# Moving nine query steps of the latent heads to a later stretch of a transformer layer on one core

## The chip, the cores and the metric

The kernel runs on one core of a Trainium2 chip. The metric is the device time of one execution in microseconds, and lower is better. A core has a matrix engine (TensorE, PE in the profile, with its weight loads on a row of their own, PEld), a vector engine (DVE), a scalar engine (ACT), a general engine (GpSimd, POOL) and a sync engine (SP). Here SP issues all loads, POOL issues all stores to DRAM, and each engine takes its instructions in a fixed order.

## The reference, cut to what matters

One layer of a streaming encoder: 1072 new rows (32 sample rows, 16 learned rows, 1024 prompt rows) and 512 cached rows of width 1024, in single precision. One input projection feeds two groups of eight heads; then an output projection, a feed-forward net and a norm.

```python
q = (rms_norm(c_q, q_norm) @ w_uq).reshape(B, L, 8, 96)          # latent heads: queries
q_mla = jnp.concatenate([q[..., :64], rope(q[..., 64:], pos)], axis=-1)
k, v = expand_mla_kv(latent, k_rope, w_ukv)                       # latent heads: keys, values
o_a = attend(take(q_mla), k_mla, v_mla, MLA_SCALE, cid[None, :] <= q_cid[:, None])
o_b = attend(take(f_q), f_k, f_v, FOX_SCALE, idx[None, :] <= q_idx[:, None], fox_bias(take(cum), cum))
x = x + concatenate([o_a, o_b]) @ w_out
return x + (silu(h @ w_gate) * (h @ w_up)) @ w_down               # h = rms_norm(x, norm_ffn)
```

## The kernel before

Every product runs in three matmuls on operands that are split into a high and a low part (`split`, L66), each matmul with 128 rows of weights and up to 512 columns. The program has three stretches: the projections (to about 240 us), the attention (to about 690 us) and the second half of the output projection with the feed-forward net (to the end).

The attention takes the eight forgetting heads first (h = 8 to 15), then the eight latent heads (h = 0 to 7). `attention` (L725) handles a head in two halves: the scores of the query tiles 5 to 8 (called 5a, 8a and so on below: head number and a), then those of tiles 1 to 4 and 0 (b). Beside the scores of one half run the values of the half before (`values`, L619: transposes L651 and L627, the products L667, L668, L637), kept in `state["pend"]`; the tile-0 transposes (L627, five at a time) are the last transposes of a head and run in the first half of the head after it. Every second head ends with `finish_pair` (L684, transposes L706), which writes that pair's rows into the operands of the output projection.

Beside this work runs a filler, a generator that makes other products in small steps. It is called by `fill()` (L728) after every score tile and every value block, some 25 times a head. Each call adds `rate` to what is owed, and for each whole step owed one step is made.

- With the forgetting heads the filler is `latent_heads` (L445), 62 steps: 16 key steps (K, six matmuls of 396 columns), 26 value steps (V, six of 256), two steps that only load, and 18 query steps (Q, nine of up to 358). The Q steps come in six blocks of three, in the order 4, 5, 0, 1, 2, 3: blocks 4 and 5 are the part of the queries that is rotated (a chain of five vector operations, L517 to L522), blocks 0 to 3 the plain part of two heads each. Between the last V step and the first Q step the operand tiles A_hi and A_lo are loaded anew (L493 to L500).
- With the latent heads it is `out_half` (L537), 48 half steps (O, six matmuls of up to 358) of the output projection over the forgetting heads' rows. They read what `finish_pair` of heads 14 and 15 writes, so `fill` makes none in the first half of head 0.

The results of the K, V and Q steps go through small buffers to DRAM: a ring of six (three tiles `room`, two buffers each) and a seventh in the tail of A_lo. The rotated blocks use only three of them in turn, since the others hold the tables. At the start of head 15 the code drains the filler, then `masks()` (L780) loads the shared rotated keys and the mask rows into the third `room` tile, where buffers 4 and 5 of the ring lie, and then `fetch(0)` (L393) loads head 0's operands. Head 0's scores need both.

The program order given so far is not the order on the engines: a planner lays out each engine's queue when the program is built, taking what comes first in the program among what its own estimates say is ready. So work whose inputs come late is overtaken by work written behind it. All pools of the attention are small: one buffer for the filler's sums (`psF`), two for scores (`psS`), two sets of head operands.

Of the kernel before, what the change touches and what calls it, by code (L numbers as in the profile page):

```python
# [42 lines left out]
RING = 6  # L43
# [6 lines left out]
def trunk(ctx: ExitStack, tc: tile.TileContext, a):  # L50
# [390 lines left out]
    psO = B.enter_context(tc.tile_pool(name="psO", bufs=1, space=PSUM))  # L441
    psF = B.enter_context(tc.tile_pool(name="psF", bufs=1, space=PSUM))
    mixed = {}

    def latent_heads():  # L445

        def weights(name, m, K, n):
            stg, hi, lo = (wp.tile([128, 512], t, tag=g, name=g)[:, :K * n].rearrange("p (k n) -> p k n", k=K)
                           for t, g in ((F32, "wst"), (FR, "woh"), (FR, "wol")))
            load(stg, a[name][m])  # L450
            split(hi, lo, stg, pool)
            return hi, lo

        hi, lo = slot("A_hi"), slot("A_lo")
        l_hi, l_lo = (t[:, :2 * NK].rearrange("p (k t) -> p k t", k=2) for t in (hi, lo))
        for c0, n in KC:
            for j, t in enumerate((l_hi, l_lo)):
                move(t[:, :, c0:c0 + n], sL[:, :, j, c0:c0 + n].rearrange("k p t -> p k t"))
        turn = [0]

        def part():

            turn[0] = (turn[0] + 1) % (RING + 1)
            return ring[turn[0]] if turn[0] < RING else lo[:, 3 * T:3 * T + 792]

        def es(n):
            return part()[:, :2 * n].rearrange("p (j t) -> p j t", j=2)

        todo = [("w_uk", m, 2, 128) for m in range(4)] + [("w_uv", m, 2, 256) for m in range(2)]
        ws = [weights(*todo[0])]  # L470
        yield
        for m in range(6):
            if m + 1 < 6:
                ws.append(weights(*todo[m + 1]))
            w = ws[m]
            if m < 4:
                for c0, n in KC:
                    ps = psF.tile([128, 512], F32, tag="psF", name="psF")
                    mm3(ps[:, :n], lambda k: w[0][:, k], lambda k: w[1][:, k],
                        lambda k: l_hi[:, k, c0:c0 + n], lambda k: l_lo[:, k, c0:c0 + n], 2)  # L480
                    spill(es, sK[m, :, :, c0:c0 + n], ps[:, :n], n)
                    yield
            else:
                for k0, n in [(128 * i, 128) for i in range(4)] + [(PAST + t0, n) for t0, n in QT]:
                    ps = psF.tile([128, 512], F32, tag="psF", name="psF")
                    for k in range(2):
                        s_hi, s_lo = l_hi[:, k, k0:k0 + 128], l_lo[:, k, k0:k0 + 128]
                        pe.matmul(ps[:, :256], s_hi, w[0][:, k], start=(k == 0), stop=False)
                        pe.matmul(ps[:, :256], s_hi, w[1][:, k], start=False, stop=False)
                        pe.matmul(ps[:, :256], s_lo, w[0][:, k], start=False, stop=(k == 1))  # L490
                    spill_v(None, k0, 4 * (m - 4), ps[:n, :256], n, part()[:, :512].rearrange("p (h d) -> p h d", h=4))
                    yield
        hi, lo = slot("A_hi"), slot("A_lo")  # L493
        c_hi, c_lo = (t[:, :3 * T].rearrange("p (k t) -> p k t", k=3) for t in (hi, lo))
        move(c_hi, sCQ[:, :, 0].rearrange("k p t -> p k t"))
        move(c_lo, sCQ[:, :, 1].rearrange("k p t -> p k t"))

        trig = [f32(ring[i][:, :716].rearrange("p (j t) -> p j t", j=2)) for i in range(3)]
        for t, (c0, n) in zip(trig, CC):
            load(t[:, :, :n], a["trig"][:, :, c0:c0 + n])  # L500
        order = (4, 5, 0, 1, 2, 3)
        ws = [weights("w_uq", order[0], 3, 128)]
        yield
        for i, m in enumerate(order):
            if i + 1 < 6:
                ws.append(weights("w_uq", order[i + 1], 3, 128))
            w = ws[i]
            for cs, (c0, n) in zip(trig, CC):
                ps = psF.tile([128, 512], F32, tag="psF", name="psF")
                mm3(ps[:, :n], lambda k: w[0][:, k], lambda k: w[1][:, k],  # L510
                    lambda k: c_hi[:, k, c0:c0 + n], lambda k: c_lo[:, k, c0:c0 + n], 3)
                if m < 4:
                    spill(es, sQ[m, :, :, c0:c0 + n], ps[:, :n], n, SCALE)
                else:
                    turn[0] = max(turn[0], 3)
                    t1, t2 = (f32(ring[3][:, 358 * j:358 * j + 358]) for j in range(2))
                    act.activation(t1[:, :n], ps[:, :n], AF.Copy, scale=SCALE)  # L517
                    dve.stream_shuffle(t2[:, :n], t1[:, :n], [(i + 16) % 32 for i in range(32)])
                    dve.tensor_tensor(out=t2[:, :n], in0=t2[:, :n], in1=cs[:, 1, :n], op=ALU.mult)
                    dve.tensor_tensor(out=t1[:, :n], in0=t1[:, :n], in1=cs[:, 0, :n], op=ALU.mult)  # L520
                    dve.tensor_tensor(out=t1[:, :n], in0=t1[:, :n], in1=t2[:, :n], op=ALU.add)
                    spill(es, sQR[m - 4, :, :, c0:c0 + n], t1[:, :n], n)  # L522
                    if turn[0] == RING:
                        turn[0] = 3
                yield

    w_ring, w_next = [], [0]

# [8 lines left out]
    def out_half():  # L537

        hi, lo = (rows4(t) for t in mixed["B"])
        turn = 0  # L540
        out_weights(1)
        for m in range(8):
            out_weights(m + 2)
            w = w_ring[m]
            for c0, n in CC:
                turn = (turn + 1) % 8
                xt = f32(ring[turn // 2][:, 396 * (turn % 2):396 * (turn % 2) + 358])
                load(xt[:, :n], a["xT"][128 * m:128 * m + 128, c0:c0 + n])
                ps = psF.tile([128, 512], F32, tag="psF", name="psF")
                for k in range(4):  # L550
                    pe.matmul(ps[:, :n], w[0][:, k], hi[:, k, c0:c0 + n], start=(k == 0), stop=False)
                    pe.matmul(ps[:, :n], w[0][:, k], lo[:, k, c0:c0 + n], start=False, stop=False)
                    pe.matmul(ps[:, :n], w[1][:, k], hi[:, k, c0:c0 + n], start=False, stop=(k == 3))
                    if k == 1:
                        yield
                dve.tensor_tensor(out=xt[:, :n], in0=ps[:, :n], in1=xt[:, :n], op=ALU.add)
                put(sX2[128 * m:128 * m + 128, c0:c0 + n], xt[:, :n])
                yield

    def scores(h, ops, i, rs):  # L560
        t0, nq = QT[i][0], 128
# [158 lines left out]
        for g in gens:  # L720
            yield from g

    state = {"pend": iter(()), "n": 0}

    def attention(hs, filler, steps, last):  # L725
        rate, owed = steps / (25.0 * (len(hs) - 0.7)), [0.0]

        def fill():  # L728
            if last and h == hs[0] and grps[0][0] == 5:
                return  # L730
            owed[0] += rate
            while owed[0] >= 1:
                next(filler, None)
                owed[0] -= 1

        rs = raw = None
        for h in hs:
# [2 lines left out]
                heads[nxt] = 0  # L740
            ops, v = heads.pop(h)
            if h == hs[-1]:
                for _ in filler:
                    pass
                if not last:
                    masks()
            nops = fetch(nxt) if nxt in heads else None
            if h % 2 == 0:
# [2 lines left out]
                raw = st.tile([128, T], F32, tag="raw", name="raw", bufs=1)  # L751
            for grps in (((5, 6, 7, 8),), ((1, 2, 3, 4), (0,))):
                todo = [i for g in grps for i in g]
                P, done = {}, 0
                for j, i in enumerate(todo):
                    P[i] = scores(h, ops, i, rs)
                    fill()
                    while done < (j + 1) * state["n"] // len(todo):
                        next(state["pend"], None)
                        fill()  # L760
                        done += 1
                for _ in state["pend"]:
                    pass
                if nops is not None and len(grps) == 1:
                    heads[nxt] = (nops, fetch_v(nxt))
                gens = [values(h, v, [(i, P[i]) for i in g], raw) for g in grps]
                state["n"] = sum(len(g) + g[0] if g != (0,) else 1 for g in grps)
                if h % 2 == 1 and len(grps) == 2:
                    gens.append(finish_pair(h // 2, rs, raw))
                    state["n"] += 3  # L770
                state["pend"] = chain(*gens)
        for _ in filler:
            pass

    mixed["B"] = (slot("B_hi"), slot("B_lo"))

# [7 lines left out]
        move(B3[96:106], sMK[0:10])  # L784
        mixed["B3"] = B3

    attention(range(8, 16), latent_heads(), 62, False)
    mixed["A"] = (slot("A_hi"), slot("A_lo"))

    attention(range(0, 8), out_half(), 48, True)  # L790
    for _ in state["pend"]:
        pass
    B.close()
# [295 lines left out]
```

## Time and profile before

| what | value |
|---|---|
| median of three runs | 1538.38 us (1536.78 to 1539.22) |
| the profiled execution's own time, and its span | 1537.25 us, 1535.5 us |
| TensorE: matmul busy, weight load busy | 1493.0 us (97%), 1433.5 us (93%) |
| VectorE, ScalarE, GpSimd busy | 971.5 (63%), 591.4 (39%), 198.5 us (13%) |
| mean granted TensorE clock | 0.993 |
| stretch of the attention | about 240 to 690 us |

The span runs from the first to the last instruction. Matmuls are pipelined and their ends are modelled, so the start of one matmul and the start of the next tell more than the durations. A line such as L67, L68 or L121 is that of a helper, so groups are told apart by the tile's name: `psF<-A_hi,woh` is a K or Q step, `psF<-woh,A_hi` a V step, `psF<-B_hi,woh` an O step, `psS<-room,x` the third score product of a latent head, which reads the masks' tile.

### The profile page before, as it was taken

What the parts mean: (1) busy time and instruction counts of PE and PEld (TensorE: products, weight loads), DVE (VectorE), ACT (ScalarE), POOL (GpSimd) and SP (SyncE); (2) the same over time, 40 slices, a digit from 0 to 9 for tenths busy, and PEclk for the clock granted to TensorE, in tenths of its full rate; (3) what the DMA queues carried; (4) which work ended last, traced back from release to release, by engine and by line L of the source; (5) the groups of instructions that cost most, each with busy time, mean ns of one, the idle gap of its engine ahead of it and who ended that gap; (6) DMA issues with size and microseconds to landing.
All of it is one profiled execution on the core that took longest, in us unless ns stands there. A gap on an engine that the chain in (4) does not pass through costs nothing.

```text
span 1535.5 us, 24295 instructions
## 1 busy us (share of the span) xinstructions
PE 1493.0 (97%) x9317; PEld 1433.5 (93%) x9317; DVE 971.5 (63%) x1861; ACT 591.4 (39%) x1198; POOL 198.5 (13%) x331
## 2 busy tenths in 40 slices
PE   9999998999898999989999999999999999999996
PEld 8999997888787898979999999999999999999996
DVE  8874626787966776766855655555555555655547
ACT  7443436777655666654511111111111121111124
POOL 0343242422131211200000000000000000000001
PEclk9999999999999999999999999999999999999999
DMA  6689567778587686515111111111111111111003
GB/s 196 233 258 299 172 210 249 238 218 262 147 238 185 174 212 161 148 41 206 34 50 44 54 42 42 42 42 42 42 42 42 53 58 53 44 42 42 28 1 115
DMA packets 87636, 184.19 MB, mean 120 GB/s; under 512 B 9754, under 2 KB 52954, under 8 KB 87428
## 3 DMA queue, kind: packets, MB, share of 16 engines
q1 hardware_dynamic: 70592, 128.34, 28.8%
q0 software_dynamic: 16928, 54.29, 10.1%
q8 instruction: 74, 1.21, 0.3%
q14 instruction: 42, 0.34, 0.1%
HBM read 123.93 MB, written 58.67 MB: 119 GB/s over the span
## 4 chain that ended last, share of the span: by engine, by line
PE 88%; DVE 4%; ACT 3%; issue 2%; DMA 1%; POOL 1%; DVEq 0%; SPq 0%; POOLq 0%; ACTq 0%
PE psG L122 11%; PE psG L121 11%; PE psG L123 11%; PE psD L890 5%; PE psD L891 5%; PE psD L889 5%; PE psS L589 5%; PE psT L651 4%; PE psA L123 3%; PE psA L121 3%; PE psA L122 3%; PE po L667 2%; PE po L668 2%; PE psA L386 1%; PE psA L387 1%
## 5 line engine op out<-in xcount | busy, mean ns | idle before, releaser
L898 DVE TENSOR_TENSOR x<-psD,x 128x408 f32<-128x408 f32 (+1 forms) x496 | 236.2, 522 | 4.3 <-PE psD L891 4.3
L122 PE MATMUL psG<-B_lo,gh 128*128 128x408 f32 (+1 forms) x528 | 172.8, 327 | 0.0
L121 PE MATMUL psG<-B_hi,gh 128*128 128x408 f32 (+1 forms) x528 | 172.8, 327 | 0.0
L122 PE MATMUL psG<-A_lo,gh 128*128 128x408 f32 (+1 forms) x528 | 172.6, 327 | 0.0
L121 PE MATMUL psG<-A_hi,gh 128*128 128x408 f32 (+1 forms) x528 | 172.3, 326 | 0.0
L891 PE MATMUL psD<-ah,dl 128*128 128x408 f32 (+1 forms) x528 | 172.1, 326 | 0.0
L123 PE MATMUL psG<-B_hi,gl 128*128 128x408 f32 (+1 forms) x528 | 171.8, 325 | 0.0
L123 PE MATMUL psG<-A_hi,gl 128*128 128x408 f32 (+1 forms) x528 | 171.8, 325 | 0.0
L890 PE MATMUL psD<-al,dh 128*128 128x408 f32 (+1 forms) x528 | 171.7, 325 | 0.0
L889 PE MATMUL psD<-ah,dh 128*128 128x408 f32 (+1 forms) x528 | 170.9, 325 | 0.5 <-ACT ah L67 0.5
L878 ACT ACTIVATE sl<-sl 128x408 f32<-128x408 f32 (+1 forms) x66 | 33.1, 503 | 351.3 <-DVE sl L877 351.2
L882 DVE TENSOR_TENSOR sq<-psG,rb 128x408 f32<-128x408 f32 (+1 forms) x66 | 35.0, 530 | 156.5 <-PE psG L123 156.5
L68 DVE TENSOR_TENSOR ptl<-psT,pth 128x512 fp32r<-128x512 f32 x192 | 104.6, 552 | 28.7 <-ACT pth L67 26.6
L592 DVE TENSOR_REDUCE nm<-psS 128x1 f32<-128x656 f32 (+2 forms) x144 | 104.0, 724 | 27.2 <-PE psS L589 25.6
L67 ACT ACTIVATE pth<-psT 128x512 fp32r<-128x512 f32 (+4 forms) x208 | 99.2, 480 | 55.7 <-PE psT L651 46.5
L830 POOL TENSOR_TENSOR acc<-acc,sq 128x408 f32<-128x408 f32 x10 | 10.8, 1076 | 812.4 <-ACT sq L829 811.9
L877 DVE TENSOR_TENSOR sl<-psG,rb 128x408 f32<-128x408 f32 (+1 forms) x66 | 34.9, 530 | 123.0 <-PE psG L123 123.0
L67 ACT ACTIVATE ah<-sl 128x408 fp32r<-128x408 f32 (+1 forms) x66 | 33.2, 503 | 197.2 <-DVE sl L883 125.8
L589 PE MATMUL psS<-b,a 128*128 128x328 f32 (+4 forms) x360 | 99.9, 331 | 7.4 <-ACT pb L597 6.1
L889 PEld LDWEIGHTS psD<-ah,dh 128*128 128x128 f32 x528 | 99.2, 188 | 0.9 <-ACT ah L67 0.7
L122 PEld LDWEIGHTS psG<-B_lo,gh 128*128 128x128 f32 x528 | 99.2, 188 | 0.5 <-issue 0.3
L121 PEld LDWEIGHTS psG<-B_hi,gh 128*128 128x128 f32 x528 | 99.2, 188 | 0.5 <-issue 0.2
(274 smaller groups left out, 3803.5 us busy)
## 6 DMA issues: line engine op xcount, KB each, us to landing
sg<-w_gu SPq DMA_DIRECT2D x44, 512.0 KB
a<-sQ SPq DMA_DIRECT2D x56, 268.0 KB
b<-sK SPq DMA_DIRECT2D x32, 396.0 KB
sg<-w_down SPq DMA_DIRECT2D x22, 512.0 KB
v<-sV SPq DMA_DIRECT2D x16, 512.0 KB
wst<-w_in SPq DMA_DIRECT2D x13, 512.0 KB
sV<-vt POOLq DMA_DIRECT2D x24, 256.0 KB, 4.5
sK<-room POOLq DMA_DIRECT2D x14, 396.0 KB, 4.9
```

The lines of the kernel that those rows point to most:

```text
L67: first = act.activation(hi, src, AF.Copy)
L68: return first.ins, eng.tensor_tensor(out=lo, in0=src, in1=f32(hi), op=ALU.subtract).ins
L121: pe.matmul(ps, whi(k), rhi(k), start=(k == 0), stop=False)
L122: pe.matmul(ps, whi(k), rlo(k), start=False, stop=False)
L123: last = pe.matmul(ps, wlo(k), rhi(k), start=False, stop=(k == K - 1))
L589: pe.matmul(out, qa[:K, t0:t0 + nq], kb[:K, k0 + c:k0 + c + w], start=(j == 0), stop=last)
L592: dve.tensor_reduce(out=nm[:nq, j:j + 1], in_=src, axis=AX.XY if len(src.shape) == 3 else AX.X, op=ALU.max, negate=True)
L651: pe.transpose(out=pt[:, 128 * g:128 * g + 128], in_=tiles[g][1][:, c:c + 128], identity=ident)
L889: pe.matmul(ps, dh[:, m], ah[:, cs], start=first and j == 0, stop=False)
L890: pe.matmul(ps, dh[:, m], al[:, cs], start=False, stop=False)
L891: pe.matmul(ps, dl[:, m], ah[:, cs], start=False, stop=last and j == len(parts) - 1)
L898: dve.tensor_tensor(out=x2[:, m, cs], in0=ps[:, :n], in1=x2[:, m, cs], op=ALU.add)
```

## The change

`latent_heads` now also yields the cost of what it has made: 1 for a step, 0 at two marks. The first mark (`state["keys"]`) stands after block 0, the second (`state["made"]`) after the last block. At the start of head 15 the filler is drained only up to the first mark; then come `masks()` and `fetch(0)` as before, and the nine steps of blocks 1, 2 and 3 are left to the paced filler of heads 15 and 0. From the first mark on the ring leaves out buffers 4 and 5. The rate of the forgetting heads follows from 53 steps in place of 62, that of the latent heads from 57 in place of 48. The filler of the latent heads is the rest of `latent_heads` and then `out_half`; in the first half of head 0 it may now run, but not past the second mark. `fill` makes a step as soon as anything is owed, not when a whole step is. The new tiles A_hi and A_lo, which `finish_pair` of heads 0 and 1 writes, are asked for in the second half of head 1.

```diff
         def part():
             turn[0] = (turn[0] + 1) % (RING + 1)
+            if state["keys"] and turn[0] in (RING - 2, RING - 1):
+                turn[0] = RING
             return ring[turn[0]] if turn[0] < RING else lo[:, 3 * T:3 * T + 792]
...
             w = ws[i]
+            if i == 3:
+
+                state["keys"] = True
+                yield 0
             for cs, (c0, n) in zip(trig, CC):
...
-                yield
+                yield 1
+        state["made"] = True
+        yield 0
...
         def fill():
-            if last and h == hs[0] and grps[0][0] == 5:
-                return
             owed[0] += rate
-            while owed[0] >= 1:
-                next(filler, None)
-                owed[0] -= 1
+            while owed[0] > 0:
+                if last and h == hs[0] and grps[0][0] == 5 and state["made"]:
+                    owed[0] = 0
+                    return
+                owed[0] -= next(filler, 1)
...
             if h == hs[-1]:
-                for _ in filler:
-                    pass
-                if not last:
+                if last:
+                    for _ in filler:
+                        pass
+                else:
+                    while not state["keys"]:
+                        next(filler)
                     masks()
...
                 todo = [i for g in grps for i in g]
+                if last and h == hs[1] and len(grps) == 2:
+                    while not state["made"]:
+                        next(filler)
+                    mixed["A"] = (slot("A_hi"), slot("A_lo"))
...
-        for _ in filler:
-            pass
...
-    attention(range(8, 16), latent_heads(), 62, False)
-    mixed["A"] = (slot("A_hi"), slot("A_lo"))
-
-    attention(range(0, 8), out_half(), 48, True)
+    first = latent_heads()
+    attention(range(8, 16), first, 53, False)
+
+    attention(range(0, 8), chain(first, out_half()), 57, True)
```

## Rows read from the trace of the kernel before

**Rows 1.** The page's busy time by engine, with shares of the span and instructions.
```profile
PE 1493.0 (97%) x9317; PEld 1433.5 (93%) x9317; DVE 971.5 (63%) x1861; ACT 591.4 (39%) x1198; POOL 198.5 (13%) x331
```
**Rows 2.** Busy time by stretch; columns as in the first line, all in us.
```profile
core 0: us, PE busy (x) PEld busy (x) DVE busy (x) ACT busy (x) POOL busy (x), PEclk, DMA share, GB/s
300.00:340.00 40.00, 39.75 (x291) 35.83 (x290) 32.25 (x67) 31.41 (x82) 12.31 (x25) 1.00 0.76 218
371.00:392.00 21.00, 19.35 (x124) 15.46 (x124) 15.72 (x31) 15.90 (x39) 2.41 (x8) 1.00 1.07 316
392.00:432.00 40.00, 35.41 (x207) 30.27 (x207) 37.12 (x74) 23.07 (x55) 11.32 (x16) 0.96 0.52 142
432.00:461.00 29.00, 26.95 (x174) 24.43 (x173) 16.88 (x36) 17.64 (x45) 11.06 (x18) 1.00 0.85 249
461.00:482.00 21.00, 16.65 (x94) 14.37 (x93) 11.45 (x22) 10.78 (x27) 4.10 (x7) 0.92 0.78 197
482.00:630.00 148.00, 145.11 (x946) 132.59 (x946) 104.88 (x198) 94.24 (x222) 30.84 (x54) 1.00 0.70 182
631.00:658.00 27.00, 26.57 (x176) 24.58 (x175) 18.02 (x34) 15.26 (x37) 5.67 (x10) 1.00 0.38 104
658.00:676.00 18.00, 16.51 (x108) 14.32 (x108) 14.31 (x28) 13.35 (x33) 0.54 (x1) 1.00 0.08 26
676.00:690.00 14.00, 9.80 (x57) 7.71 (x56) 9.71 (x21) 6.73 (x16) 1.84 (x6) 0.88 0.09 24
```
**Rows 3.** TensorE in order of time: the last V step, two heads' ends, the first Q step.
```profile
368.94 0.28 PE L490 MATMUL psF<-woh,A_lo 128*128 128x256 f32 x1
...
371.50 0.76 PE L627 MATMUL psT<-ident,pa 128*112 128x128 f32 x5 [0.79 <-DVE ptm L656]
...
387.67 0.41 PE L121 MATMUL psF<-A_hi,woh 128*128 128x358 f32 x1
...
390.61 0.72 PE L627 MATMUL psT<-ident,pa 128*112 128x128 f32 x5
```
**Rows 4.** TensorE: where the second, seventh, ninth and eighteenth Q steps begin.
```profile
395.03 0.33 PE L121 MATMUL psF<-A_hi,woh 128*128 128x358 f32 x1
...
422.72 0.43 PE L121 MATMUL psF<-A_hi,woh 128*128 128x358 f32 x1
...
430.46 0.34 PE L121 MATMUL psF<-A_hi,woh 128*128 128x356 f32 x1
...
459.17 0.43 PE L121 MATMUL psF<-A_hi,woh 128*128 128x356 f32 x1 [0.19 <-DVE room L144]
```
**Rows 5.** The SP queue in order of time: loads for head 0, and the masks.
```profile
438.32 1.95 SPq L61 DMA_DIRECT2D a<-sQ  x3
...
440.88 0.44 SPq L61 DMA_DIRECT2D a<-sQ  x1
...
459.40 1.24 SPq L61 DMA_DIRECT2D room<-sKR  x3
```
**Rows 6.** SP's longest wait from 425 to 475 us: total, times, longest.
```profile
SPq L61 <- DMA sQ<-room: 13.7, 2, 8.2
```
**Rows 7.** TensorE behind the last Q step, and at head 0's first scores.
```profile
460.73 0.39 PE L667 MATMUL po<-pth,v 128*128 128x512 f32 x1
...
469.01 0.43 PE L551 MATMUL psF<-B_hi,woh 128*128 128x358 f32 x1 [1.25 <-ACT B_hi L713]
...
469.89 0.32 PE L589 MATMUL psS<-room,x 106*128 106x328 f32 x1
```
**Rows 8.** TensorE: a V step and what follows it; two O half steps and what follows.
```profile
304.34 0.28 PE L488 MATMUL psF<-woh,A_hi 128*128 128x256 f32 x1
...
305.04 0.60 PE L651 MATMUL psT<-ident,pb 128*128 128x128 f32 x4
...
655.78 0.43 PE L551 MATMUL psF<-B_hi,woh 128*128 128x356 f32 x1
...
657.84 0.34 PE L589 MATMUL psS<-room,x 106*128 106x392 f32 x1
```

More of the change, by code (lines that the diff above doesn't have):

```diff
@@ L443, in trunk @@
     mixed = {}
+    state = {"pend": iter(()), "n": 0, "keys": False, "made": False}
     def latent_heads():
@@ L481, in latent_heads @@
                     spill(es, sK[m, :, :, c0:c0 + n], ps[:, :n], n)
-                    yield
+                    yield 1
             else:
@@ L491, in latent_heads @@
                     spill_v(None, k0, 4 * (m - 4), ps[:n, :256], n, part()[:, :512].rearrange("p (h d) -> p h d", h=4))
-                    yield
+                    yield 1
         hi, lo = slot("A_hi"), slot("A_lo")
@@ L502, in latent_heads @@
         ws = [weights("w_uq", order[0], 3, 128)]
-        yield
+        yield 1
         for i, m in enumerate(order):
@@ L524, in latent_heads @@
                         turn[0] = 3
-                yield
+                yield 1
+        state["made"] = True
+        yield 0
     w_ring, w_next = [], [0]
@@ L554, in out_half @@
                     if k == 1:
-                        yield
+                        yield 1
                 dve.tensor_tensor(out=xt[:, :n], in0=ps[:, :n], in1=xt[:, :n], op=ALU.add)
                 put(sX2[128 * m:128 * m + 128, c0:c0 + n], xt[:, :n])
-                yield
+                yield 1
     def scores(h, ops, i, rs):
@@ L721, in chain @@
             yield from g
-    state = {"pend": iter(()), "n": 0}
     def attention(hs, filler, steps, last):
```

## The prediction

> **What bounds the kernel now.** The page's busy table comes first: TensorE is busy 97% of the span, no other engine over 63% [rows 1]. So in most stretches time goes only where TensorE idles, and the sum of its work is the same after the change: not one matmul is added or removed. The question is where it idles, and the busy time by stretch answers it [rows 2]. From 300 to 340 us and from 482 to 630 us, where a filler runs beside the heads, the weight loads are busy 35.83 of 40 and 132.59 of 148 us, 0.896 both times. I take 0.896 as a full TensorE; what a stretch has less, over 0.896, is lost time. So 371 to 392 loses 21 - 15.46/0.896 = 3.7 us, 392 to 432 loses 6.2, 432 to 461 loses 1.7, 461 to 482 loses 5.0, 631 to 658 nothing (-0.4), 658 to 676 loses 2.0 and 676 to 690 loses 5.4. The changed part thus holds some 16.6 us between 371 and 482, and the end of the attention 7.4.
>
> The queues in order of time tell what those losses are. The last V step is at 368.94 and the first Q step at 387.67 [rows 3]: 18.7 us without filler, while A_hi, A_lo, the tables and the weights are loaded anew. Then the six rotated steps run 5.5 us apart (second to seventh step, 395.03 to 422.72, five gaps) and the plain ones 3.2 us apart (ninth to eighteenth, 430.46 to 459.17, nine gaps) [rows 4]. VectorE is busy 37.12 of 40 us from 392 to 432 [rows 2]: the rotation's chain of operations stands among the softmax work. At 461 the forgetting heads have run out. Head 0's last operand is issued at 440.88, but the masks only at 459.40 [rows 5], since their tile is the ring's buffers 4 and 5, whose last stores are those of block 2; SP waited 8.2 us for such a store [rows 6]. Head 0's first product with the masks starts at 469.89, and TensorE idles around it, 1.25 us in one piece [rows 7].
>
> **The change, part by part.**
>
> *Where the steps go.* Some 25 calls a head make the rates 62, 48, 53 and 57 over 182.5: 0.340 and 0.263 a call before, 0.290 and 0.312 after. The last V step is the 43rd step: call 127 before, and 145 after, as a step now comes when anything is owed (42/0.290). These 18 calls are 0.7 of a head; a head without filler took 19.1 us (371.50 to 390.61) [rows 3], of which 16 were work, so the V steps end 11.4 to 13.4 us later; I take 12.5. Everything tied to them moves with them: loads of A, rotated steps, block 0, sQ for head 0. Of the nine plain steps about seven fall to head 15 and two to head 0 by count.
>
> *Gain at head 0.* After block 0 the ring skips buffers 4 and 5, so the masks wait for block 0's own first two stores, not for block 2. Head 0's operands then bound it: 440.88 + 12.5 = 453.4, some 455.5 with the landing. TensorE would be out of other work near 461 (the last Q step ended at 460.73) [rows 7]. By 455.5 the plain steps, 3.2 us apart from about 446 on (the tenth, at 430.46 + 3.2 + 12.5), have come to three or four; five or six are left to lie beside head 0's first scores, 1.56 us each (459.17 to 460.73) [rows 4, 7], 8 to 9 us of work where 5.0 us was idle. The stretch 461 to 482 also had a granted clock of 0.92 [rows 2], that is half clock for 0.16 of 21 us, 1.7 us of lost work. Recovered: 5.0 + 1.7 = 6.7 us at most, and nothing at least. Stretch 432 to 461, the same plain steps beside heads, loses 6%, so I leave 0.9 of some 15 us: -5.8 us.
>
> *Cost of thinner filling in heads 8 to 13.* At call 127 the changed kernel has made 37 steps (127 x 0.290) where 42 stood, so 5 V steps fewer, each 0.70 us (304.34 to 305.04) [rows 8]: 3.5 us of work. If TensorE is what limits those heads, the work is only moved and the cost is 0; if not, it is 3.5. A head without filler needs 19.1 us, one with 7.3 V steps 16 + 5.1 = 21.1 of TensorE, so it stays the limit; some bursts will miss. I take 0.8.
>
> *Cost at the end.* 48 half steps at 0.312 a call last 154 calls, six heads from the middle of head 0, so they end in the first half of head 6. Before they ended at 657.84, ten of them after 631, 1.03 us each (655.78 to 657.84, two) [rows 8]. Without them 631 to 658 holds 27 - 10.3 = 17 us of attention alone. A forgetting head without filler loses 3.7 of 21 us, 18%; latent heads, with three products a score, lose 2.0 of 18, 11% [rows 2], and part of that is the scores running out. So 0 to 3.0 us, and I take 1.6. The drain of five half steps at head 7 goes; it cost nothing, since 631 to 658 is full.
>
> *No change costed:* the stretch without filler (18.7 us, now beside head 14 in place of 13b and 14a) and the rotated steps (now beside head 15), 3.7 and 6.2 us as before. The new ring of five buffers for the nine plain steps has 5 x 3.2 = 16 us a turn against a longest SP wait of 8.2 us for a store [rows 4, 6], so it hides; without that cover it would cost a few us of waits at the filler. The marks and the early step issue nothing. The masks' and head 0's loads stand earlier in SP's queue; the loads behind them are those of head 1, not wanted for another 10 us. A_hi and A_lo for `finish_pair` are asked for later but used only in head 2.
>
> *How far matmul busy time can be trusted* is the Trainium skill's point in "Trainium Kernel Development and Optimization", Performance Expectations: matmul busy time is a bad measure because matmuls are pipelined, weight-load busy time a good one. This trace agrees: from 392 to 432 matmuls look 89% busy, weight loads 76% against 90% in a full stretch [rows 2]. By matmul busy time 461 to 482 would have 4.35 us to give in place of 5.0, and the whole 0.65 us less gain.
>
> **Sum.** -5.8 + 0.8 + 1.6 = -3.4 us. The profiled execution took 1537.25 us, of which the span is 1535.5; it would take 1533.85. The median of the runs shown is 1.13 us above it, so 1535.0 us, 0.22% under the 1538.38 of before. About 0.2% (3.1 us) is what a measurement can tell here, so the forecast lies at that edge.
>
> **Rivals.**
>
> *More than head 0 is repaired* (faster). The rotated steps no longer meet the pair's end of heads 12 and 13 (it falls into the stretch without filler), and VectorE, nearly full from 392 to 432, gets room. For it: the clock was 0.96 there, 1.6 us of lost work. Against it: the chain of a rotated step is the same and still behind softmax work. If half of 6.2 + 1.6 goes: 1535.0 - 3.9 = 1531.1.
>
> *The gain is given back at the end or halved at the start* (no change). If head 6 and 7 without filler cost 3.0 and a spell of half clock (676 to 690 shows 0.88, 1.7 us of 14, once the scores had run out [rows 2]), the sum is -5.8 + 0.8 + 4.7 = -0.3: 1538.1. If the planner puts the nine steps ahead of head 0 in place of beside it, as before, half of the 5.8 goes: -0.5, 1537.9. Against the first: 658 to 676 ran without filler at 1.00. "TensorE: Matmul & The Clock Gate", What's actually happening, of the Trainium skill has the clock throttled unless activity releases it, which speaks against a longer thin end; this trace shows no fall before the scores end.
>
> *The late chain decides* (slower). All of block 4, 5 and 0 now lies 12.5 us later, and head 0 waits for it. From the last V step to head 0's last issue took 440.88 - 368.94 = 72 us [rows 3, 5]. If that is longer beside head 15, because VectorE has 93% to do already [rows 2], TensorE finds neither scores nor a ready step. It decides from the point where the operands come after 461, some 6 us late: a pace of 6.6 in place of 5.5 us for the six rotated steps would do. Then nothing of the 6.7 us comes back, the 2.4 us of thinner filling and empty end stay, and each further us of lateness adds one: with 2.5, 1538.4 + 2.4 + 2.5 = 1543.3. For it: the stretch without filler costs the same, and the loads of head 15 may delay those of A.
>
> *The steps do not move:* if the planner's estimates let the nine steps run where they did, the masks still come earlier; that is the forecast with a smaller gain, within the second rival.
>
> **How the numbers follow.** Forecast 0.38, with 1532.5 to 1537 as its own range (0.27 of it faster, 0.11 within 0.2%); more repaired 0.19 (faster); given back 0.26 (0.23 the same, 0.03 slower); late chain 0.17 (0.14 slower, 0.03 the same). That is faster 0.46, same 0.37, slower 0.17. The range reaches past the second case's 1531.1 to 1529.5 and up to 1540.5, short of the late chain's 1543.3; what it leaves out is some 0.07 below and 0.12 above.
>
> **What would show it.** Right: the masks' load follows the store of block 0's second step; head 0's first product with the masks starts near 456 to 458, with Q steps among its scores; the stretch to the start of head 0's values has weight loads near 0.87; the last O half step comes in the first half of head 6. Wrong: idle time before `psS<-room` as before, or a gap between Q steps and head 0 with VectorE full; a clock under 1 between the last O step and the end of the scores; or a loss of over 2 us in heads 8 to 13.

## The result and the profile after

The changed kernel takes 1548.95 us (median of five runs, 1546.58 to 1553.02) against 1538.64 us for the kernel before in the same session: ratio 1.0068, 95% interval 1.0057 to 1.0079, so 10.3 us slower. The profiled execution took 1546.58 us, its span 1544.8; that is 9.3 us over the profiled execution of before.

The page's busy table shows the same work to within 3 us [rows 1]. So the time is idle time on TensorE, as the prediction argued, and again the question is where.

```profile
PE 1490.7 (96%) x9317; PEld 1430.6 (93%) x9317; DVE 971.0 (63%) x1861; ACT 591.0 (38%) x1198; POOL 199.4 (13%) x331
```

Busy time by stretch, after; columns as in the first line. The stretches are cut where the phases of the changed kernel begin, so they answer to [rows 2] as sums, not line by line.

```profile
core 0: us, PE busy (x) PEld busy (x) DVE busy (x) ACT busy (x) POOL busy (x), PEclk, DMA share, GB/s
300.00:340.00 40.00, 38.87 (x274) 34.18 (x275) 32.08 (x65) 29.75 (x77) 10.29 (x21) 1.00 0.77 212
371.00:386.00 15.00, 15.00 (x114) 13.76 (x113) 11.54 (x26) 11.42 (x32) 4.25 (x11) 1.00 0.63 181
386.00:411.00 25.00, 22.14 (x143) 17.55 (x141) 20.03 (x38) 19.17 (x47) 4.69 (x8) 1.00 1.06 305
411.00:446.00 35.00, 30.38 (x188) 25.52 (x187) 30.20 (x69) 21.10 (x53) 8.25 (x13) 1.00 0.51 142
446.00:476.00 30.00, 19.13 (x106) 16.32 (x105) 8.64 (x18) 7.46 (x16) 10.42 (x17) 1.00 0.90 274
476.00:488.00 12.00, 10.09 (x59) 8.50 (x57) 7.02 (x14) 7.38 (x19) 4.53 (x6) 1.00 0.67 216
488.00:624.00 136.00, 132.40 (x865) 122.44 (x865) 93.96 (x174) 81.86 (x193) 30.32 (x51) 1.00 0.69 173
649.00:676.00 27.00, 24.30 (x159) 21.21 (x158) 21.08 (x40) 19.14 (x45) 4.05 (x7) 1.00 0.21 56
676.00:692.00 16.00, 14.21 (x92) 11.61 (x93) 11.94 (x26) 11.54 (x31) 1.43 (x4) 1.00 0.01 2
```

With the prediction's measure (weight loads over 0.896 is what TensorE needed), 446 to 476 loses 30 - 16.32/0.896 = 11.8 us, the largest loss by far. From 371 to 488 the loss is -0.4 + 5.4 + 6.5 + 11.8 + 2.5 = 25.8 us. Before, 371 to 482 lost 16.6 us and 3.3 more by its lower clock, 19.9 [rows 2]. That is +5.9 us. From 488 to 624 nothing is lost.

TensorE in order of time, after:

```profile
370.78 0.76 PE L636 MATMUL psT<-ident,pa 128*112 128x128 f32 x5 [0.16 <-DVE ptm L665]
...
384.46 0.29 PE L493 MATMUL psF<-woh,A_lo 128*128 128x256 f32 x1
...
410.92 0.41 PE L121 MATMUL psF<-A_hi,woh 128*128 128x358 f32 x1
...
444.62 0.43 PE L121 MATMUL psF<-A_hi,woh 128*128 128x358 f32 x1 [0.18 <-ACT room L524]
...
446.19 0.40 PE L674 MATMUL po<-ptm,v 128*128 128x512 f32 x1
447.75 0.44 PE L121 MATMUL psF<-A_hi,woh 128*128 128x358 f32 x1 [1.16 <-DVE room L144]
...
449.34 0.66 PE L646 MATMUL po<-pth,v 112*128 112x96 f32 x5
...
454.19 0.43 PE L121 MATMUL psF<-A_hi,woh 128*128 128x358 f32 x1 [1.84 <-DVE A_lo L144]
...
471.64 0.43 PE L121 MATMUL psF<-A_hi,woh 128*128 128x358 f32 x1 [1.12 <-DVE room L144]
...
473.21 0.50 PE L598 MATMUL psS<-b,a 128*128 128x328 f32 x2
...
475.90 0.31 PE L598 MATMUL psS<-room,x 106*128 106x328 f32 x1
...
698.77 0.42 PE L858 MATMUL psG<-A_hi,woh 128*128 128x408 f32 x1 [1.36 <-DVE raw L721]
```

The last V step is at 384.46, where it was at 368.94 [rows 3]; the first Q step at 410.92 (387.67); the seventh, the first plain one, at 444.62 (422.72) [rows 4]. The forgetting heads' last products stand at 446.19 and 449.34. From there seven of the nine moved steps, the tenth to the sixteenth, run alone, one each 2.9 us (454.19 to 471.64, six gaps), for 1.7 us of matmuls. Only behind the sixteenth comes head 0's first product, at 473.21, and the first one with the masks at 475.90, 6 us later than before [rows 7].

What TensorE waits for from 446 to 476 (us in total, times, longest):

```profile
PE psF L121 <- DVE room L144: 7.9, 8, 1.4
PE psF L121 <- DVE A_lo L144: 3.0, 2, 1.8
```

There is one buffer `psF`: a step can't start until ScalarE has copied the sum of the step before and VectorE has split it. Beside attention work that wait is filled; alone it stands as 1.1 us a step, 10.9 us in all.

The SP queue after, the load of A_hi, two loads behind it, the masks and the last load that head 0's first scores need:

```profile
388.15 0.38 SPq L61 DMA_DIRECT2D A_hi<-sCQ  x1
...
397.31 8.34 SPq L61 DMA_DIRECT2D v<-sV  x4
405.75 0.37 SPq L58 DMA_DIRECT2D wst<-w_uq  x1
...
456.98 1.23 SPq L61 DMA_DIRECT2D room<-sKR  x3
...
460.78 0.58 SPq L61 DMA_DIRECT2D a<-sQ  x1
```

The same queue before (not shown so far), and below it TensorE's first product of the feed-forward net before:

```profile
369.13 0.38 SPq L61 DMA_DIRECT2D A_hi<-sCQ  x1
...
379.18 3.88 SPq L61 DMA_DIRECT2D v<-sV  x4
```

```profile
688.81 0.68 PE L845 MATMUL psG<-A_hi,woh 128*128 128x408 f32 x1 [1.10 <-DVE raw L712]
```

The masks now come 2.4 us earlier than before (456.98 against 459.40 [rows 5]), but the last operand 19.9 us later (460.78 against 440.88; eight loads `a<-sQ` start from 458.72 to 463.71, and in the program's order the first four are head 0's, the others head 1's). The feed-forward net starts 10.0 us later, and that accounts for the whole difference.

### The profile page after: what moved, and what is told of

It reads as the page before. It is cut to its first block, busy times and chain, and to the rows that moved or that the text cites. A ratio compares the mean times of both kernels' runs of the same rounds, so it can differ in the third digit from the quotient of the medians.

```text
span 1544.8 us, 24294 instructions
## 1 busy us (share of the span) xinstructions
PE 1490.7 (96%) x9317; PEld 1430.6 (93%) x9317; DVE 971.0 (63%) x1861; ACT 591.0 (38%) x1198; POOL 199.4 (13%) x331
## 4 chain that ended last, share of the span: by engine, by line
PE 87%; DVE 5%; ACT 5%; issue 1%; DMA 1%; SPq 0%; POOL 0%; DVEq 0%; ACTq 0%
PE psG L122 11%; PE psG L121 11%; PE psG L123 11%; PE psD L903 5%; PE psD L904 5%; PE psD L902 5%; PE psS L598 5%; PE psT L660 4%; PE psA L123 3%; PE psA L121 3%; PE psA L122 3%; PE po L676 2%; PE po L677 2%; ACT pb L606 1%; PE psA L386 1%
```

## The experiments

The main theory: the late chain decides. Everything from the last V step to head 0's operands comes later than the forgetting heads' work lasts. Rivals: the order in which the planner queues the nine steps ahead of head 0, the thinner filling of heads 8 to 13 and of the end, and the step made as soon as anything is owed.

**The chain early, the rest of the change kept.** 62 steps' pace again, with the filler held at the first mark until head 15.

```diff
             while owed[0] > 0:
+                if not last and state["keys"] and h != hs[-1]:
+                    owed[0] = 0
+                    return
...
-    attention(range(8, 16), first, 53, False)
+    attention(range(8, 16), first, 62, False)
```

> The changed kernel with the forgetting heads' pace put back to 62 steps, and the filler held at the first mark until head 15, so that the V steps end and A is loaded at the calls of before, and the same nine Q steps are left to heads 15 and 0. Late chain (head 0 waits for blocks 4, 5 and 0): the last V step is back near 369 us, no run of Q steps stands alone ahead of head 0, and the time falls by some 12 us, to 1535 to 1538. Thin filling of heads 8 to 13 as the cause: only the 4 us that those heads lost come back, 1545. The moved steps or the ring of five buffers as the cause: no change, 1547 to 1550.

Measured 1536.49 us, ratio 0.9990 (0.9979 to 1.0000): 12.5 us under the changed kernel, even with the kernel before or slightly faster. The first store of a rotated query (on POOL) comes at 403.56 where the changed kernel has 424.92, and head 0's first product with the masks at 459.08:

```profile
403.56 0.71 POOL L64 DMA_DIRECT2D sQR<-room  x1 [3.32 <-DVE nm L601]
...
459.08 0.39 PE L598 MATMUL psS<-room,x 106*128 106x328 f32 x1
```

So lateness, with the thinner filling that goes with it, is all of the slowdown.

**The end's pace.** The changed kernel with 49 for 57 in the latent heads.

```diff
-    attention(range(0, 8), chain(first, out_half()), 57, True)
+    attention(range(0, 8), chain(first, out_half()), 49, True)
```

> The changed kernel with the latent heads' pace at 49 steps in place of 57, so that the O steps end at head 7 and not in head 6. Late chain: only the end is repaired, 1.8 us, 1547. Empty end as the main cause: 1541 or less.

Measured 1546.43 us, ratio 1.0054 (1.0036 to 1.0071), 2.5 us under the changed kernel, though the two intervals overlap. The trace agrees: the last matmul of the O steps starts at 665.7 in place of 652.6, and 649 to 676 loses 27 - 23.52/0.896 = 0.75 us in place of 3.3:

```profile
649.00:676.00 27.00, 25.78 (x168) 23.52 (x168) 19.06 (x38) 17.53 (x44) 4.95 (x7) 1.00 0.25 79
```

**The masks early, alone.** The kernel before with the first mark, the shorter ring and the masks' load behind block 0; all 18 Q steps are drained at head 15 as before, with the rates of before and a step for each whole share.

```diff
                     masks()
+                    for _ in filler:
+                        pass
...
-    attention(range(8, 16), first, 53, False)
+    attention(range(8, 16), first, 62, False)
-    attention(range(0, 8), chain(first, out_half()), 57, True)
+    attention(range(0, 8), out_half(), 48, True)
```

> Before, with one part of the change: the mark behind block 0, the ring without buffers 4 and 5 from there on, and the masks loaded at the mark; but all 18 Q steps still drained at the start of head 15, paces 62 and 48, a step for each whole share. Late chain: the chain is as early as before and the masks no longer hold head 0, so the 6 us around 461 to 482 us come back and it is faster than before, 1532 to 1534. If the five buffers or the masks' place cost what the change lost, it is slower than before, 1541 or more; if the idle time at head 0 had another cause, 1538.

Measured 1536.18 us, ratio 0.9987 (0.9975 to 0.9998). The masks are issued at 435.57 in place of 459.40, head 0's first product with them starts at 460.85 in place of 469.89, and 461 to 482 loses 21 - 16.77/0.896 = 2.3 us at full clock, where it lost 5.0 and 1.7 by the clock. But 482 to 530, part of a stretch that lost nothing before [rows 2], now loses 3.35:

```profile
461.00:482.00 21.00, 19.22 (x127) 16.77 (x126) 15.98 (x30) 15.30 (x38) 4.17 (x7) 1.00 0.64 198
482.00:530.00 48.00, 45.09 (x281) 40.01 (x281) 30.49 (x60) 28.05 (x68) 11.47 (x19) 1.00 0.66 163
```

So the repair of head 0 is worth 4.4 us where it is made, and some 2 us in the time.

**The query weights first.** The changed kernel with the first w_uq weights asked for ahead of A_hi and A_lo.

```diff
+        order = (4, 5, 0, 1, 2, 3)
+        ws = [weights("w_uq", order[0], 3, 128)]
         hi, lo = slot("A_hi"), slot("A_lo")
...
-        ws = [weights("w_uq", order[0], 3, 128)]
```

> The changed kernel with the first w_uq weights asked for ahead of the loads of A and of the tables, so that SP issues them before head 15's values. Late chain through SP's queue: the first rotated step's store moves from 424.7 to about 416 us and the time falls by 6 to 8 us, 1541 to 1543. Late chain through the V steps alone: 1547 to 1550. Thin filling: the same, 1547 to 1550.

Measured 1549.53 us, ratio 1.0076 (1.0055 to 1.0097): nothing. Those weights had been early already: the first three of the six loads `wst<-w_uq` stand at 301.27, 301.74 and 350.51 in the changed kernel, and the one at 405.75 is the fourth. The edit moved nothing in time, so it speaks neither for nor against the loads as the cause of the wide gap between V and Q.

**The steps beside head 0.** The changed kernel with all nine plain steps left to head 0, their matmuls queued behind head 0's first score tile.

```diff
+                with tc.issue_after(state["gate"]) if i >= 3 else ExitStack():
+                    mm3(ps[:, :n], ...)
...
             while owed[0] > 0:
+                if not last and state["keys"]:
+                    owed[0] = 0
+                    return
```

> The changed kernel, but the nine steps of blocks 1 to 3 are all made in head 0 and their matmuls are queued on TensorE behind head 0's first score tile; everything up to block 0 keeps its place. If the nine steps standing alone ahead of head 0 cost the time: head 0's first product with the masks moves from 475.9 us to when its operands have landed, near 464, the steps fall beside the scores, and the time falls by 4 to 8 us, to 1541 to 1545. If head 0 waits for its operands anyway and the steps alone cost nothing: it starts no sooner than 473 and the time stays at 1548 or rises.

Measured 1549.71 us, ratio 1.0072 (1.0059 to 1.0085); no gain, so the expectation failed, though head 0's first product with the masks starts at 469.72, 6 us sooner. TensorE finishes block 0 at 453 and then stands 12.47 us for head 0's operands; the second fence is the stretch around it, with half clock in much of it, and below it the part from the first product to the end of the half clock:

```profile
453.03 0.33 PE L123 MATMUL psF<-A_hi,wol 128*128 128x356 f32 x1
465.82 0.61 PE L599 MATMUL psS<-b,a 128*128 128x328 f32 x1 [12.47 <-DMA a<-sQ]
```

```profile
453.00:470.00 17.00, 3.66 (x16) 2.96 (x15) 1.21 (x2) 1.62 (x3) 2.69 (x5) 0.66 0.98 244
465.80:472.00 6.20, 5.31 (x20) 4.89 (x20) 1.53 (x2) 0.71 (x2) 1.68 (x3) 0.50 1.03 234
```

This is the hole itself, with the steps taken out of it: the first operand comes at 465.8, and without the plain steps TensorE has nothing left from 453 on. The 6.2 us at half clock cost at most 3.1 us of work, so the run leaves it open whether the planner's order is worth that much; it is not the cause of the 10.3 us. The second of the two loads that this product needs was issued at 460.28, 5.5 us before it starts:

```profile
460.28 0.60 SPq L61 DMA_DIRECT2D a<-sQ  x1
```

**The sum freed early.** The changed kernel with the low parts of blocks 1 to 3 made from the high part's own tile (they are zeros), so `psF` is free after ScalarE's copy.

```diff
-                    spill(es, sQ[m, :, :, c0:c0 + n], ps[:, :n], n, SCALE)
+                        act.activation(t[:, 0], ps[:, :n], AF.Copy, scale=SCALE)
+                        dve.tensor_tensor(out=t[:, 1], in0=f32(t[:, 0]), in1=f32(t[:, 0]), op=ALU.subtract)
```

> The changed kernel, but in the steps of blocks 1 to 3 VectorE no longer reads the sum: the low parts of these queries are left out (zeros), so the one buffer of the filler's sums is free after ScalarE's copy. If the steps that stand alone are paced by that buffer: their gap of 1.1 us falls to about 0.6, the pace from 2.9 to 2.3 us, and nine of them give 4 to 5 us, 1544 to 1545. If the pace is set by something else (weights, stores, the ring of five): no change, 1548 to 1550.

Measured 1545.81 us, ratio 1.0046 (1.0032 to 1.0060): 3.1 us under the changed kernel, less than expected. The wait of a step falls from 1.12 to 0.56 us and the pace from 2.9 to 2.3 us:

```profile
457.52 0.43 PE L121 MATMUL psF<-A_hi,woh 128*128 128x358 f32 x1 [0.56 <-ACT room L524]
```

So the single sum's turn is a part of the price of the hole, not its cause.

**Whole shares.** The changed kernel with `while owed[0] >= 1`.

> The changed kernel with the old rule that a step is made only when a whole one is owed; all else as changed. Each step comes about 3.4 calls later. Late chain: the last V step and all behind it move 2 to 3 us later, 1549 to 1552. If the early step was the fault (steps ahead of the scores that they displace): faster than the changed kernel, 1546 or less.

Measured 1548.87 us, ratio 1.0068 (1.0048 to 1.0087), though the last V step came 3.8 us later still (388.25) and the first rotated store 1.35 us later (426.27): that part of the change has no price that shows.

**Without the reload.** The changed kernel without the loads of A_hi and A_lo ahead of the Q steps (the queries are made from what the tiles hold, and are not the reference's).

```diff
-        move(c_hi, sCQ[:, :, 0].rearrange("k p t -> p k t"))
-        move(c_lo, sCQ[:, :, 1].rearrange("k p t -> p k t"))
```

> The changed kernel without the loads of A_hi and A_lo for the Q steps: these read what the K and V steps left there, so the latent heads' queries are not the reference's. This takes away the wait between the last V step and the first Q step (26.5 us in the changed kernel, 18.7 before), with the pace of 53 as it is. Late chain: blocks 4, 5 and 0 end 10 to 20 us sooner, head 0's operands land before TensorE runs out of other work, and the time falls by 8 to 12 us, to 1537 to 1541. Thin filling or the moved steps as the cause: 1546 or more.

Measured 1542.30 us, ratio 1.0029 (1.0017 to 1.0040): 6.6 us under the changed kernel, less than expected. The first Q step follows the V steps at once (388.35), but the third comes only at 411.55. Its sum's buffer waits for the rotation of the first, whose products with the tables stand at 408.11 in VectorE's queue; the tables go into the ring's tiles, whose V stores must be out first, and were asked for at 394.31. So there is a second leg behind the reload, and the first rotated store comes at 413.36, not near 403. By the trace's record of landings the first table was there by 397.7, and VectorE was on other work, with waits under 1 us, up to 408: what set 408.11 is the place of those products in VectorE's fixed order, not the landing. The first rotated store:

```profile
413.36 0.71 POOL L64 DMA_DIRECT2D sQR<-room  x1 [11.54 <-PE psF L123]
```

With the first rotated store at 403.6, 413.4 and 424.9 (the early chain, this kernel, the changed kernel) the times are 1536.5, 1542.3 and 1549.0: some 0.6 us for each us of lateness, the thinner filling included.

**Lateness put into the kernel before.** Six empty steps among the last 13 V steps, nothing else changed.

```diff
+                    if m == 5 and k0 == 384:
+                        for _ in range(6):
+                            yield
```

> Before, with one thing added: six empty steps ahead of the fifth of the last thirteen V steps, so that the last V step and all Q steps come some 18 calls later, as in the changed kernel; paces, drain and masks as before, nothing moved to head 0. Late chain: head 0's operands and masks come 15 to 20 us later and TensorE waits for them; slower than before by 10 to 20 us, 1549 to 1558. If the thinner pace or the moved steps were the cause, the lateness alone costs little: 1538 to 1542.

Measured 1555.45 us, ratio 1.0117 (1.0103 to 1.0131): lateness by itself costs 17 us there, where the masks still wait for block 2. Little of it is thinner filling: 340 to 371 has 25.75 us of weight loads against 26.37 before. The masks go out at 481.55 and head 0's first product with them starts at 489.53, 22 and 20 us later [rows 5, 7]:

```profile
481.55 0.79 SPq L61 DMA_DIRECT2D room<-sKR  x2
...
489.53 0.31 PE L592 MATMUL psS<-room,x 106*128 106x328 f32 x1
```

Its last V step stands at 383.77 and its first Q step at 412.30, 28.5 us apart:

```profile
383.77 0.28 PE L493 MATMUL psF<-woh,A_lo 128*128 128x256 f32 x1
...
412.30 0.33 PE L121 MATMUL psF<-A_hi,woh 128*128 128x358 f32 x1
```

So the wider gap comes with the place where the V steps end, not with any other part of the change.

**Early chain and late end together, and earlier still.** The first experiment with 49 for 57 in the latent heads, then with 66 for 62 in the forgetting ones.

> Both repairs: the forgetting heads' pace at 62 with the filler held at the first mark (as in the run with the early chain, 1536.5), and the latent heads' pace at 49. If the end's loss adds to the chain's: 2 to 2.5 us under the early chain alone, 1534 to 1534.5, faster than before. If the early chain has already taken it: 1536.5.

> The version with both repairs (1535.5), with the forgetting heads' pace at 66 in place of 62: the V steps end some 8 calls earlier still. If what is left of the loss at head 0 (3.3 us around 450 to 460) is still the chain: 1 to 3 us faster, 1532.5 to 1534.5. If the chain no longer binds: 1535 to 1536; if the filler now runs dry in head 14: slower, 1537.

Measured 1535.50 us, ratio 0.9984 (0.9976 to 0.9993), and 1535.64 us, ratio 0.9983 (0.9974 to 0.9992). Both beat the kernel before by some 2.5 us, and the changed kernel by 13. In the second the first rotated store comes at 385.59, 17 us ahead of the kernel before, and that gives nothing more; 440 to 460 still loses 20 - 14.12/0.896 = 4.2 us:

```profile
385.59 0.70 POOL L64 DMA_DIRECT2D sQR<-room  x1 [3.85 <-DVE room L525]
```

```profile
440.00:460.00 20.00, 16.90 (x112) 14.12 (x111) 13.88 (x28) 11.92 (x28) 4.02 (x11) 1.00 0.78 199
```

**The output weights earlier.** The masks-early kernel, with the weights of the first O steps asked for ahead of block 3.

```diff
             w = ws[i]
+            if i == 5:
+                out_weights(1)
```

> The kernel with early masks alone (e3_masks_only, 1536.2 us) and one edit more: the output step's weights of the next group are asked for at the sixth latent head's turn ahead of the place where they stand now, so that the first O step can run among head 0's scores, as it did before (463 us), and not at 488. Theory that the stretch 482 to 530 us lost its 3.35 us because the O steps had no weights: that stretch's loss falls to about 1, the first O step comes before 475, and the time is 1533.0 to 1534.8. Rival, that the stretch lost because the work that filled it was spent earlier, whatever the weights: the O steps come earlier, but the loss only moves, later heads get thinner, and the time stays at 1535.5 to 1537.

Measured 1535.88 us, ratio 0.9983 (0.9973 to 0.9992), the same as without the edit. The first O step comes at 467.12 in place of 488, and 461 to 482 loses 1.45 us, but 482 to 530 now 4.6:

```profile
467.12 0.37 PE L562 MATMUL psF<-B_hi,woh 128*128 128x358 f32 x1
```

```profile
461.00:482.00 21.00, 19.94 (x133) 17.52 (x132) 15.24 (x30) 15.24 (x37) 4.18 (x7) 1.00 0.58 183
482.00:530.00 48.00, 44.16 (x276) 38.88 (x277) 31.77 (x63) 28.11 (x69) 10.46 (x19) 1.00 0.69 172
```

The theory of the late weights falls; the loss only moves, as the rival said. Why this stretch runs at 90 to 93% of a full TensorE once head 0 starts earlier stays open.

## Why the prediction was wrong

The forecast was 1535.0 us, faster; what happened is the rival "The late chain decides", and by more than its 1543.3.

**The step that failed** is "TensorE would be out of other work near 461 (the last Q step ended at 460.73)". That row is the last of the plain steps. They come behind block 0 and so move with the late chain: they are no work that TensorE has until block 0 is done, and alone they keep it busy for 1.7 of 2.9 us. Without them the forgetting heads' work ends at 446.19 to 449.34, and with the plain steps taken out of the way TensorE stands from 453 on. The rival's own condition, "from the point where the operands come after 461, some 6 us late", took the same wrong time; the true one is some 10 us earlier, so that even the forecast lateness of 12.5 us was past it. Its chance of 0.17 was too small for that reason. In place of a gain of 5.8 us, 371 to 488 lost 5.9 us more than 371 to 482 did before.

**The chain was also later than forecast.** Head 0's last operand was issued at 460.78, not 453.4. These 7.4 us are 3.0 from the V steps (15.5 us later against 12.5) and 7.7 from the gap between the last V step and the first Q step (26.5 against 18.7), costed as unchanged, less 3.3: from the first Q step to that load it took 49.9 us, against 53.2 before. So the reason that the rival gave for more lateness, rotated steps at 6.6 us because VectorE is full, did not come (5.2 us a step, 418.44 to 444.62, five gaps; VectorE is busy 8.64 of 30 us in the hole): that the rival had the direction right is in part luck. Of the 7.7, A_hi's load takes 3.5: it is issued 3.7 us after the last V step, behind the operand loads of the next head, against 0.2 before. The other 4.2 aren't told apart; the transfers are full both times (DMA share 1.06 at 305 GB/s from 386 to 411, 1.07 at 316 before [rows 2]). The prediction had named this ("the loads of head 15 may delay those of A") in the rival only. Without the reload the gap shrinks to 4 us, and 6.6 us of the time come back. The prediction's time for the landing was too short as well: it allowed 2.1 us (453.4 to 455.5), and in the run with the steps behind head 0's scores the first operand took 5.5.

**Of the gain at head 0**, 8 to 9 us of work where 5.0 was idle, nothing came. The steps did move, in part: seven of them stand in one row ahead of head 0's first product, at 2.9 us each, and putting them beside its scores gave no gain either, since the first operand came at 465.8 and half clock took up to 3.1 us. Nor was the term 5.8 us where the chain is early: the masks-early kernel gains 4.4 there and gives 3.35 back by 530; its median is some 2 us under the kernel before. The step "Recovered: 5.0 + 1.7" counted a stretch's loss as the kernel's.

**Thinner filling:** forecast 0.8 of at most 3.5, and 2.3 by these rows. Before, the transposes that end head 12 start at 371.50 with all 26 V steps done [rows 3]; after, the same start at 370.78 with 21.7 done. That is 4.3 x 0.70 = 3.0 us less work, and only 0.7 us sooner. In the stretch 300 to 340, 1.85 us are lost where nothing was.

**The end:** forecast 1.6 of at most 3.0. Of the 10.0 us at the feed-forward net's start, 2.3 and 5.9 are spoken for, so 1.8 is left for it; the experiment on the pace gives 2.5. There was no fall of the clock before the scores ended (1.00 from 649 to 692), as the forecast had it. The five-buffer ring, costed at nothing, doesn't show apart from the single sum.

**Two readings that do not hold**, with little weight in the sum. The 8.2 us of rows 6 is SP's wait ahead of head 0's operands (427 to 436 us); the one ahead of the masks is the other, 5.5 us (450 to 460):

```profile
SPq L61 <- DMA sQ<-room: 8.2, 1, 8.2
SPq L61 <- DMA sQ<-room: 5.5, 1, 5.5
```

And by the prediction's own count 43 steps, not 42, stood at call 127, so six V steps were fewer there, 4.2 us and not 3.5.

**What was right:** the same work, so only idle time counts; the masks' load (456.98) follows block 0 and no longer block 2; the terms for filling and end by mechanism and within their bounds; no price for the step made early.

## What to carry to other kernels

When a filler makes the operands of the next stage, its pace is a due date: slowing it to share work with the next stage moves the whole chain behind it, and here each us of lateness cost some 0.6 between the early chain and the changed kernel, while a chain 17 us earlier than before gave nothing more. To find when an engine runs out of other work, strike from the trace all work that itself depends on the late chain, and only then look for the last row. And the loss in a stretch is an upper bound of a repair, since work done earlier there is missing later.

## What was not expected of the hardware

TensorE's granted clock stayed at 1.00 (2.4 GHz) from 446 to 476 us in the profiled execution of the changed kernel, where TensorE worked in pieces of 1.7 us with waits of 1.1. In the run with the query weights first the same pieces and waits stand in the trace, and there it was at half (1.2 GHz) from 454.2 to 461.0:

```profile
454.20:461.00 6.80, 5.43 (x18) 4.50 (x16) 0.53 (x1) 0.68 (x2) 1.22 (x2) 0.50 0.86 248
```

So one execution does not tell which level such a stretch gets. In the experiment with one idle time of 12.47 us it was 0.66 on average from 453 to 470, that is half clock for some 0.68 of it.

The issue of the four loads of values on SP took 8.34 us in the changed kernel and 3.88 in the kernel before, of which 1.5 is a wait for GpSimd. One such issue took between 0.54 and 3.93 us after, and between 0.42 and 2.22 before:

```profile
L61 SPq DMA_DIRECT2D v<-sV x4: 542/1833/3932, 397.3 to 405.1; - x4
L61 SPq DMA_DIRECT2D v<-sV x4: 417/521/2222, 379.2 to 382.6; - x4
```

The DMA share was 1.06 and 1.03 in these two stretches, so it does not tell why.
